# Half of x loaded already transposed, small inputs packed, and the loads at the start put over two queues

## The chip, the cores and the metric

One NeuronCore of one Trainium2 chip runs the whole program. Its engines work side by side and each in its own fixed order: TensorE (PE, matmuls and transposes), VectorE (DVE), ScalarE (ACT), GpSimd (POOL) and SyncE (SP, which here only issues DMAs). The metric is the device time of one execution in microseconds; the time of a version is the median of its runs.

## The reference, cut to what matters

Two pre-norm residual layers on x of 256 positions by 2048 features, all float32. Layer 0 is sliding-window attention with sinks, layer 1 a sparse attention with three branches. The change touches the first things that layer 0 computes: the norm, the projection, and the rotation tables.

```
def rmsnorm(x, g):
    y = xf * lax.rsqrt(jnp.mean(xf * xf, axis=-1, keepdims=True) + NORM_EPS)
    return y * g
def mixer_a(h, w_in, sinks, w_out, cos, sin):
    q, k, v, z = jnp.split(h @ w_in, ...)
    q, k = apply_rope(q, cos, sin), apply_rope(k, cos, sin)   # first 16 of 64 dims
    o = banded_attention(q, k, v, A_WINDOW, A_QBLOCK, sinks)
    return (o * jax.nn.silu(z)) @ w_out
for i in range(2):
    x = x + mixer(rmsnorm(x, norm_w[i]), ...)
return rmsnorm(x, final_norm_w)
```

## The kernel before, in words

**Matmuls.** Each projection multiplies h (256 x 2048) by a weight matrix, over 16 K-tiles of 128 features. A float32 number is split in two parts, hi and lo, which TensorE takes at the speed of its fp32r type, and a product takes three matmuls: hi by hi, lo by hi, hi by lo. Weights come in steps of 512 KB (`load`, line 544): two K-tiles by 512 columns in a tile `raw`, of which there are four. `split` (line 549) makes the parts: ACT copies `raw` to `w_hi`, DVE subtracts and writes `w_lo` (three buffers each). A step then has 12 matmuls of 128x512, six for each half of the positions, into the banks `acc0` and `acc1`.

**The first block.** Steps 0 to 7 compute keys and values (96 matmuls). Step i needs the two K-tiles 2i and 2i+1 of h transposed, features on partitions. `hT_pair` (line 523) makes them: PE transposes two K-tiles of x in four transposes into a bank `xT`, ACT multiplies by the norm weight `gT` and writes the hi part into `hT`, DVE writes the lo part. The row factor of the norm is left out here and multiplied in behind the projection. The banks `xT` come from a ring of two (`t_bank`, line 357), so a third pair's transposes wait until ACT and DVE have read the first pair. `first_block` (line 862) calls `hT_pair` one step ahead, places the squares for the norm (`square`, ACT, line 502) at steps 4 to 7, and behind them the row factor: `scales` (DVE and a power on POOL) and `scale_rows` (two transposes into `rbc`).

**Loads at the start.** SP issues constants `cst` (identity matrix and rope frequencies), norm weights `nw`, then x in column blocks of 512 (`load_x`, line 386; two DMAs of 256 KB each, one for each half of the positions) in turn with the weights of steps 0 to 3. POOL issues positions and sinks. DVE and ACT compute the rope tables from them before the first weights are split.

**What sets the order.** Nothing runs as written: every call is recorded (`Plan.record`), given a price (`_price`, line 165) and dependencies, and a list scheduler (`Plan.order`) emits each engine's instructions in the order of its own simulated time. The engines then keep that order on the chip, and wait for exact semaphores. Dependencies between recorded calls are found by boxes: a view that is sliced keeps the box of its first slice when it is rearranged and sliced again. DMAs take one of eight semaphores in turn, and a DMA waits until the eighth before it has landed.

Of the kernel before, what the change touches and what calls it, by code (L numbers as in the profile page):

```python
# [163 lines left out]
def _price(eng, method, args, kw, out, ins):  # L164

    n = math.prod(out.shape[1:]) if out is not None else 0
    if eng == "PE":
        lhs = args[1] if len(args) > 1 else kw["lhsT"]
        r = lhs.dtype == F32R
        if lhs.dtype == BF16:  # L170
            return (n / 1.2 + 2, 0)
        if method == "transpose":
            return (out.shape[-1] * (1 if r else 2) / 2.4 + 2, 0)
        if r:
            return (max(n, 256) / 2.4 + 2, 0)
        return (n * (4 if out.shape[0] > 64 else 2) / 2.4 + 2, 0)
    if method == "dma_start":
        return (1050 if eng == "POOL" else 60, 2200)
    ptrs = sum(isinstance(kw.get(k), View) for k in ("scale", "bias", "scalar", "scalar1"))
    ptrs += sum(isinstance(a, View) and math.prod(a.shape[1:]) == 1 and n > 2 for a in args[1:])  # L180
    psum = any(v.base.psum for v in ins)
    if eng == "ACT":
        return (0.833 * n + (51 if psum else 93) + 93 * ptrs + (93 if "accum_out" in kw else 0), 0)
    if eng == "DVE":
        fast = method in ("tensor_copy", "tensor_scalar") and not psum
        m = max(n, *(math.prod(v.shape[1:]) for v in ins)) if ins else n / 2
        return ((0.52 if fast else 1.042) * m + 69 + 61 * ptrs + 10, 0)
    return (1.667 * n + 185 + (300 if kw.get("op") == OP.pow else 0), 0)
# [148 lines left out]


@with_exitstack
def trunk(ctx: ExitStack, tc: tile.TileContext, x, positions, norm_w, final_norm_w,  # L340
          a_w_in, a_sinks, a_w_out, b_w_in, kc_pos, kc_w1, kc_w2, vc_pos, vc_w1, vc_w2,
          b_w_out, consts, out):
    nc = tc.nc
    plan = Plan()
    PE, ACT, DVE, POOL, SP = (Engine(plan, n, e) for n, e in (
# [24 lines left out]
    DVE.memset(warm, 0.0)  # L370
    ACT.activation(warm, warm, AF.Sin)
    ps = s_bank("idle")
    for _ in range(9):
        PE.matmul(ps, idle[:, 0:P], idle, start=True, stop=True)


    pos_i = sb.tile([P, NT], I32, name="pos_i")
    POOL.dma_start(pos_i, dram(positions, 0, [[1, P], [P, NT]]))
    cst = sb.tile([P, P + 8], F32, name="cst")
    SP.dma_start(cst, dram(consts, 0, [[CW, P], [1, P + 8]]))  # L380
    ident = cst[:, 0:P]
    nw = sb.tile([32, 512], F32, tag="q32", name="nw", bufs=2)[:, 0:P]
    SP.dma_start(nw, dram(norm_w, 0, [[P, 32], [1, P]]))
    xt = [sb.tile([P, D], F32, name=f"x{t}") for t in range(NT)]

    def load_x(j):
        for t in range(NT):
            SP.dma_start(xt[t][:, j * NB:(j + 1) * NB], dram(x, t * P * D + j * NB, [[D, P], [1, NB]]))

    load_x(0)  # L390
    sinks = sb.tile([P, 32], F32, name="sinks")
    POOL.dma_start(sinks, dram(a_sinks, 0, [[0, P], [1, 32]]))

# [6 lines left out]
    posf = sb.tile([P, NT], F32, name="posf")  # L400
    DVE.tensor_copy(posf, pos_i)
    ang = sb.tile([P, NT, 8], F32, name="ang")
    for t in range(NT):
        DVE.tensor_scalar(ang[:, t], cst[:, P:P + 8], posf[:, t:t + 1], None, op0=OP.mult)
    red = sb.tile([P, 2, NT, 8], F32, name="red")
    rnd = sb.tile([P, 2, NT, 8], F32, name="rnd")
    for i, shift in enumerate((0.0, 0.25)):
        DVE.tensor_scalar(rnd[:, i], ang, 1.0 / (2.0 * math.pi), shift, op0=OP.mult, op1=OP.add)
        DVE.tensor_scalar(rnd[:, i], rnd[:, i], MAGIC, None, op0=OP.add)
        DVE.tensor_scalar(rnd[:, i], rnd[:, i], -MAGIC, None, op0=OP.add)  # L410
        src = ang
        for c in TWO_PI:
            DVE.scalar_tensor_tensor(red[:, i], rnd[:, i], -c, src, op0=OP.mult, op1=OP.add)
            src = red[:, i]
        if i:
            DVE.tensor_scalar(red[:, i], red[:, i], math.pi / 2, None, op0=OP.add)
# [4 lines left out]
    ACT.activation(sn[:, :, 1, :], red[:, 0], AF.Sin)
    ACT.activation(cs[:, :, 0, :], red[:, 1], AF.Sin)
    DVE.tensor_copy(cs[:, :, 1, :], cs[:, :, 0, :])
    DVE.tensor_scalar(sn[:, :, 0, :], sn[:, :, 1, :], -1.0, None, op0=OP.mult)

# [22 lines left out]
    nsink = sb.tile([P, 32], F32, name="nsink")  # L448
    DVE.tensor_scalar(nsink, sinks, -1.0, None, op0=OP.mult)

    gT = sb.tile([P, 32], F32, name="gT")
    tb = t_bank("nwT")
# [69 lines left out]

    def hT_pair(i, hT, j):

        tb = t_bank("xT")
        for k in range(2):
            for t in range(NT):
                PE.transpose(tb[:, 2 * k + t, :], xt[t][:, (2 * j + k) * P:(2 * j + k + 1) * P], ident)
        src = [tb[:, 2 * k:2 * k + 2, :].rearrange("p a b -> p (a b)") for k in range(2)]
# [14 lines left out]
    def load(st):  # L544
        raw = sb.tile([P, 1024], F32, tag="raw", name="raw", bufs=4)
        st.raw = raw
        st.dma(raw)

    def split(st):
        n = st.cols  # L550
        plan.early = FIRST
        st.hi, st.lo = st.room() if hasattr(st, "room") else (
            sb.tile([P, 1024], F32R, tag=tag, name=tag, bufs=3) for tag in ("w_hi", "w_lo"))
        parts = 2 if st.idx < 2 else 1
        for c in range(parts):
# [763 lines left out]
def _consts():  # L1319
# [10 lines left out]
    for g in range(NG):  # L1330
# [25 lines left out]
```

## Time and profile before

| | us |
|---|---|
| median of 3 runs | 799.94 (799.88 to 800.97) |
| profiled execution, time | 801.18 |
| its span, first to last instruction | 799.5 |
| PE busy | 783.0 (98%) |
| DVE busy | 553.8 (69%) |
| ACT busy | 479.1 (60%) |
| POOL busy | 125.5 (16%) |
| HBM read and written | 125.91 MB and 2.10 MB |

Engines overlap, so the busy times don't add up to the span. A matmul's busy time includes its way through the array; the pace of a row of them is read from their starts. The granted clock in the profile is what the throttle reports; at the start of a program, before it has reported anything, it reads 1.00, and the pace of the matmuls tells more.

### The profile page before, as it was taken

To read this page: it belongs to the slowest core of one execution; us is meant where nothing else is said; L and a number is where in the kernel's file an instruction comes from. 1 tells how busy PE (TensorE), PEld (TensorE's weight loads), DVE (VectorE), ACT (ScalarE), POOL (GpSimd) and SP (SyncE) were. 2 spreads that over 40 slices of the span, in tenths; PEclk is the share of its full clock that TensorE was granted. 3 is DMA by queue.
4 is the path that set the end of the run, shared out by engine and by line. 5 is a ranking of instruction groups with operands and counts; after the bars stand their busy time and mean duration, and the time that the engine had idled before them with its cause. 6 is when DMAs were issued, how large, how long until landed. Compare 5 with 4: busy or idle time off the path is not lost.

```text
span 799.5 us, 11784 instructions
## 1 busy us (share of the span) xinstructions
PE 783.0 (98%) x4092; PEld 631.8 (79%) x4092; DVE 553.8 (69%) x1148; ACT 479.1 (60%) x963; POOL 125.5 (16%) x169
## 2 busy tenths in 40 slices
PE   7999999999999999999999999999999999999995
PEld 4888878788788788888878887778868768777884
DVE  5657958858779655556756478858959868885572
ACT  6658657557476445554756486667658748654452
POOL 2102311213023000020101021111211021120110
PEclk9999999999999999999999999999999999999999
DMA  8655454654653555566667653544444444364652
GB/s 271 186 181 162 131 185 129 183 159 117 180 178 132 177 185 185 182 192 172 197 204 218 184 159 106 159 109 130 132 131 134 109 127 133 109 208 131 189 181 105
DMA packets 85995, 128.77 MB, mean 161 GB/s; under 512 B 6178, under 2 KB 43265, under 8 KB 85808
## 3 DMA queue, kind: packets, MB, share of 16 engines
q1 hardware_dynamic: 85536, 126.72, 52.4%
q0 software_dynamic: 400, 1.30, 0.6%
q8 instruction: 32, 0.52, 0.3%
q14 instruction: 27, 0.22, 0.1%
HBM read 125.91 MB, written 2.10 MB: 160 GB/s over the span
## 4 chain that ended last, share of the span: by engine, by line
PE 92%; DVE 3%; issue 2%; ACT 1%; DMA 1%; POOL 1%; SPq 0%; ACTq 0%; POOLq 0%; DVEq 0%
PE acc L217 75%; PE pv L217 5%; PE s L217 4%; PE pT L217 4%; PE qT L217 1%; DVE w_lo L217 1%; PE xT L217 1%; DMA raw<-in_a_w_in 1%; DVE sm L217 1%; ACT w_hi L217 1%; PE gates L217 1%; PE pcT L217 0%; PE kT L217 0%; PE mlp L217 0%; POOL rope L217 0%
## 5 line engine op out<-in xcount | busy, mean ns | idle before, releaser
L217 DVE TENSOR_TENSOR w_lo<-raw,w_hi 128x1024 fp32r<-128x1024 f32 (+1 forms) x231 | 294.0, 1275 | 154.8 <-ACT w_hi L217 151.7
L217 ACT ACTIVATE w_hi<-raw 128x1024 fp32r<-128x1024 f32 (+1 forms) x231 | 242.0, 1050 | 186.0 <-PE acc L217 149.3
L217 PE MATMUL acc<-w_hi,hT 128*128 128x512 f32 x768 | 247.6, 398 | 2.3 <-ACT w_hi L217 1.7
L217 PE MATMUL acc<-hT,w_hi 128*128 128x512 f32 x512 | 186.4, 399 | 0.0
L217 PEld LDWEIGHTS acc<-w_hi,hT 128*128 128x128 f32 x768 | 142.9, 189 | 37.9 <-issue 4.9
L217 PE MATMUL acc<-w_lo,hT 128*128 128x512 f32 x384 | 152.1, 396 | 0.0
L217 PE MATMUL acc<-hT,w_lo 128*128 128x256 f32 x512 | 143.7, 283 | 0.0
L217 PEld LDWEIGHTS acc<-hT,w_hi 128*128 128x128 f32 x512 | 96.2, 188 | 21.3 <-issue 3.2
L217 PEld LDWEIGHTS acc<-hT,w_lo 128*128 128x128 f32 x512 | 96.6, 189 | 0.7
L217 PE MATMUL acc<-w_hi,aT_hi 128*128 128x512 f32 x236 | 92.9, 394 | 0.8 <-ACT aT_hi L217 0.8
L217 PE MATMUL acc<-w_hi,aT_lo 128*128 128x512 f32 x236 | 92.6, 392 | 0.2 <-DVE aT_lo L217 0.2
L217 PE MATMUL acc<-w_lo,aT_hi 128*128 128x512 f32 x236 | 92.1, 391 | 0.0
L217 PEld LDWEIGHTS acc<-w_lo,hT 128*128 128x128 f32 x384 | 72.7, 189 | 18.5 <-issue 4.9
L217 ACT ACTIVATE sm<-sm,nmb 128x128 f32<-128x128 f32 (+1 forms) x128 | 56.9, 445 | 15.7 <-DVE nmb L217 15.1
L217 DVE CUSTOM_DVE_ANT_0 sm<-s,mask 128x128 f32<-128x128 f32 (+1 forms) x128 | 44.1, 349 | 20.6 <-PE s L217 20.4
L217 PEld LDWEIGHTS acc<-w_hi,aT_hi 128*128 128x128 f32 x236 | 44.3, 188 | 13.4 <-issue 2.4
L217 POOL TENSOR_TENSOR sm<-sm,denb 128x512 f32<-128x512 f32 (+1 forms) x16 | 29.3, 1832 | 151.2 <-DVE mx L217 60.8
L217 PEld LDWEIGHTS acc<-w_lo,aT_hi 128*128 128x128 f32 x236 | 44.3, 188 | 9.7 <-issue 0.8
L217 PEld LDWEIGHTS acc<-w_hi,aT_lo 128*128 128x128 f32 x236 | 44.3, 188 | 9.2 <-DVE aT_lo L217 0.5
L217 PE MATMUL s<-kTB,qT 128*128 128x272 f32 x192 | 39.2, 295 | 0.0
L217 PE MATMUL pT<-cst,sm 128*128 128x128 f32 x256 | 37.9, 275 | 0.5 <-DVE sm L217 0.2
L217 PEld LDWEIGHTS s<-kTB,qT 128*128 128x128 f32 x192 | 31.8, 188 | 7.4 <-issue 3.2
(187 smaller groups left out, 885.3 us busy)
## 6 DMA issues: line engine op xcount, KB each, us to landing
raw<-in_b_w_in SPq DMA_DIRECT2D x88, 512.0 KB, 3.7
raw<-in_a_w_in SPq DMA_DIRECT2D x72, 512.0 KB, 3.6
raw<-in_a_w_out SPq DMA_DIRECT2D x32, 512.0 KB, 3.6
raw<-in_b_w_out SPq DMA_DIRECT2D x32, 512.0 KB, 4.2
x<-in_x SPq DMA_DIRECT2D x8, 256.0 KB, 7.0
raw<-in_b_cmp_k_w SPq DMA_DIRECT2D x4, 512.0 KB, 3.8
raw<-in_b_cmp_v_w SPq DMA_DIRECT2D x4, 512.0 KB, 3.8
out<-x SPq DMA_DIRECT2D x4, 512.0 KB, 3.1
```

The source lines that it names most:

```text
L217: return getattr(eng.real, method)(*[real(a) for a in args], **{k: real(a) for k, a in kw.items()})
```

## The change

Half of x (K-tiles 0 to 7) comes from the host once more as `xT`, laid out by feature, and is loaded into `xf`, a tile in the room of `aT_hi`, in four DMAs of 256 KB, two K-tiles each. `hT_pair` takes those K-tiles from `xf` in place of transposes; x itself is still loaded whole. Norm weights, sinks, positions and frequencies come packed in one input `small` (128 x 74). ACT's queue issues `small` and the two halves of step 0's weights; all else stays on SP, and POOL issues none of them. POOL builds the identity matrix. The squares and the rope tables are tied to later steps. A tenth idle matmul stands at the start, and the planner's price for a DMA that is not issued by POOL is 450 in place of 60 ns.

```
-        return (1050 if eng == "POOL" else 60, 2200)
+        return (1050 if eng == "POOL" else 450, 2200)
...
-    for _ in range(9):
+    for _ in range(10):
         PE.matmul(ps, idle[:, 0:P], idle, start=True, stop=True)
...
-    POOL.dma_start(pos_i, dram(positions, 0, [[1, P], [P, NT]]))
-    SP.dma_start(cst, dram(consts, 0, [[CW, P], [1, P + 8]]))
-    SP.dma_start(nw, dram(norm_w, 0, [[P, 32], [1, P]]))
+    small_t = sb.tile([P, SMALL], F32, name="small")
+    ACT.dma_start(small_t, small)
+    gT = small_t[:, 0:32]
...
+    xf = sb.tile([P, KT * S], F32, tag="aT_hi", name="xf")[:, 0:XT * S].rearrange("p (k s) -> p k s", k=XT)
...
-    load_x(0)
-    POOL.dma_start(sinks, dram(a_sinks, 0, [[0, P], [1, 32]]))
+    def load_xf(k0, k1):
+        SP.dma_start(xf[:, k0:k1, :], dram(xT, k0 * S, [[XT * S, P], [S, k1 - k0], [1, S]]))
+    ident = sb.tile([P, P], F32, name="ident")
+    POOL.memset(ident, 1.0)
...
+    def rope_tables(later):
+        DVE.tensor_scalar(nsink, sinks, -1.0, None, op0=OP.mult).deps.add(later.i)
...
-    PE.transpose(tb[:, 0, 0:32], nw, ident[0:32, 0:32])
-    copy(gT, tb[:, 0, 0:32])
...
-        tb = t_bank("xT")
...
+        if i == 0 and 2 * j < XT:
+            src = [xf[:, 2 * j + k, :] for k in range(2)]
+        else:
+            tb = t_bank("xT")
...
+        if st.idx == 0:
+            for k in range(2):
+                ACT.dma_start(raw[:, k * NB:(k + 1) * NB],
+                              dram(a_w_in[0], k * P * A_IN + 2048, [[A_IN, P], [1, NB]]))
+            return
...
-                    square(0, t, i - 4)
+                    square(0, t, (i - 2) % 4).deps.add(steps[i + 1].ops[0].i)
+            if i == 5:
+                rope_tables(steps[i + 1].ops[1])
...
-        if i + 1 < 4:
-            load_x(i + 1)
+        if 2 * i < XT:
+            load_xf(2 * i, 2 * i + 2)
...
+        if i < 4:
+            load_x((i + 2) % 4)
```

The emitted order moves at three places. The first is SP's queue at the start. Before, constants, norm weights and x stand ahead of the first weights:

```order
L217 DMA cst<-in_consts 128x136
L217 DMA nw<-in_norm_w 32x128
L217 DMA x_67<-in_x 128x512
L217 DMA x_68<-in_x 128x512
L217 DMA raw<-in_a_w_in 128x2x512
```

After that a pair of x and one `raw` took turns. Now the queue begins with the first `xf` and the weights of steps 1 to 3, and goes on so:

```order
L217 DMA x_67<-in_x 128x512
L217 DMA x_68<-in_x 128x512
L217 DMA x_67<-in_x 128x512
L217 DMA x_68<-in_x 128x512
L217 DMA xf<-in_xT 128x512
L217 DMA x_67<-in_x 128x512
L217 DMA x_68<-in_x 128x512
L217 DMA x_67<-in_x 128x512
L217 DMA x_68<-in_x 128x512
L217 DMA raw<-in_a_w_in 128x2x512 x3
L217 DMA xf<-in_xT 128x512 x2
L217 DMA raw<-in_a_w_in 128x2x512 x9
```

The second `xf` stands behind half of x, and the third and fourth behind the rest of x and the weights of steps 4 to 6.

The second place is ACT in the first block (`junk` are the squares, `w_hi` the weights' hi parts, `hT` the hi parts of h). Before:

```order
L217 ACTIVATE hT<-xT,gT 128x256
L217 ACTIVATE w_hi<-raw 128x512 x2
L217 ACTIVATE hT<-xT,gT 128x256 x3
L217 ACTIVATE junk,ssq_103<-x_67 128x512
L217 ACTIVATE junk,ssq_103<-x_68 128x512
L217 ACTIVATE w_hi<-raw 128x512 x2
L217 ACTIVATE hT<-xT,gT 128x256 x2
```

Now:

```order
L217 ACTIVATE w_hi<-raw 128x512 x3
L217 ACTIVATE w_hi<-raw 128x1024
L217 ACTIVATE w_hi<-raw 128x512
L217 ACTIVATE hT<-xf,small 128x256 x8
L217 ACTIVATE hT<-xT,small 128x256 x3
L217 ACTIVATE w_hi<-raw 128x1024
L217 ACTIVATE hT<-xT,small 128x256 x3
```

The weights of steps 0 to 2 are copied first; then all eight K-tiles of `xf` stand in a row, and behind them the first transposed ones and the weights of step 3. DVE's lo parts follow in the same order.

The third place is PE at its third group of transposes (numbers tell the banks apart: `acc0` and `acc1` are the two halves of the positions, `xT` with a number one bank of transposes). Before, the third and fourth group stood inside step 0:

```order
L217 MATMUL acc0_221<-w_hi_70,hT_63 128x512
L217 MATMUL acc0_221<-w_lo_71,hT_63 128x512
L217 MATMUL xT_240<-cst_91,x0_67 128x128
L217 MATMUL xT_240<-cst_91,x1_68 128x128
L217 MATMUL xT_240<-cst_91,x0_67 128x128
L217 MATMUL xT_240<-cst_91,x1_68 128x128
L217 MATMUL acc0_221<-w_hi_70,hT_63 128x512 x2
```

Now `xT_196` and `xT_201` (K-tiles 8 to 11) are transposed before the first matmul, and `xT_259`, which takes the bank of `xT_196`, stands in step 1, behind nine of its twelve matmuls:

```order
L217 MATMUL acc1_219<-w_hi_180,hT_63 128x512 x2
L217 MATMUL acc1_219<-w_lo_183,hT_63 128x512
L217 MATMUL xT_259<-ident_87,x0_67 128x128
L217 MATMUL xT_259<-ident_87,x1_68 128x128
L217 MATMUL xT_259<-ident_87,x0_67 128x128
L217 MATMUL xT_259<-ident_87,x1_68 128x128
L217 MATMUL acc1_219<-w_hi_180,hT_63 128x512 x2
L217 MATMUL acc1_219<-w_lo_183,hT_63 128x512
```

Sixteen of 32 transposes of layer 0 are gone; of those left, eight stand before the first matmul as before, four in step 1 and four in step 2. In the rest of the program the engines' orders are the same but for a few places where two neighbours have changed turns.

## Rows read from the trace of the kernel before

**Rows 1.** The page's chain of work that ended last, by engine.

```profile
PE 92%; DVE 3%; issue 2%; ACT 1%; DMA 1%; POOL 1%; SPq 0%; ACTq 0%; POOLq 0%; DVEq 0%
```

**Rows 2.** Busy time by stretch: start:end length, then each engine's us (instructions), clock, DMA.

```profile
0.00:10.07 10.07, 6.42 (x18) 2.76 (x18) 3.30 (x25) 4.38 (x12) 4.16 (x16) 1.00 0.70 183
10.07:38.87 28.80, 28.29 (x122) 22.83 (x123) 19.72 (x34) 19.98 (x41) 2.32 (x4) 1.00 0.78 249
38.87:780.00 741.13, 737.43 (x3906) 597.58 (x3905) 526.42 (x1080) 450.65 (x904) 117.92 (x149) 1.00 0.53 159
```

**Rows 3.** PE in order of time: start us, length, what, count, idle before and releaser.

```profile
6.79 1.54 PE L217 MATMUL xT<-cst,x 128*128 128x128 f32 x6 [0.65 <-DMA x<-in_x]
10.07 1.22 PE L217 MATMUL acc<-w_hi,hT 128*128 128x512 f32 x2 [1.75 <-ACT w_hi L217]
11.80 0.79 PE L217 MATMUL acc<-w_hi,hT 128*128 128x512 f32 x1 [0.50 <-DVE hT L217]
...
17.46 0.40 PE L217 MATMUL acc<-w_lo,hT 128*128 128x512 f32 x1
...
41.61 0.46 PE L217 MATMUL kT<-identr,kstack 128*128 128x128 f32 x4
```

**Rows 4.** The chain of waits in the first 60 us: start, length, what, count.

```profile
13.87 0.85 PE acc L217 x2
...
26.98 0.44 PE xT L217 x4
...
29.48 12.29 PE acc L217 x54
```

**Rows 5.** SP's first DMA issue, in order of time.

```profile
0.81 0.38 SPq L217 DMA_DIRECT2D cst<-in_consts  x1
```

**Rows 6.** Busy time by stretch as in rows 2; the last two columns are DMA share and GB/s.

```profile
1.50:2.00 0.50, 0.50 (x2) 0.15 (x1) 0.26 (x1) 0.50 (x1) 0.50 (x1) 1.00 0.32 47
0.00:4.00 4.00, 2.74 (x7) 1.01 (x8) 0.77 (x4) 1.49 (x2) 2.85 (x11) 1.00 0.41 87
4.00:8.00 4.00, 3.35 (x12) 1.75 (x10) 1.88 (x16) 1.53 (x5) 1.31 (x7) 1.00 0.80 164
8.00:12.00 4.00, 1.75 (x5) 0.70 (x4) 2.58 (x8) 3.29 (x9) 0.00 (x0) 1.00 1.05 403
12.00:18.00 6.00, 6.00 (x20) 4.87 (x21) 4.02 (x8) 5.72 (x15) 0.00 (x0) 1.00 1.05 387
```

**Rows 7.** DMA queues between 4 and 8 us: packets, MB, share of the 16 DMA engines.

```profile
q1 hardware_dynamic: 334, 0.64, 45.5%
q0 software_dynamic: 57, 0.02, 34.8%
```

**Rows 8.** DMA issues of the first 60 us: size, median us from issue to landing.

```profile
pos_i<-in_positions POOLq DMA_DIRECT2D x1, 1.0 KB, 4.7
sinks<-in_a_sinks POOLq DMA_DIRECT2D x1, 16.0 KB, 5.8
```

**Rows 9.** ACT, POOL and DVE in order of time, 21 to 25 us.

```profile
21.55 0.62 ACT L217 ACTIVATE junk<-x 128x512 f32<-128x512 f32 x1
...
22.16 1.05 ACT L217 ACTIVATE w_hi<-raw 128x1024 fp32r<-128x1024 f32 x1
...
23.11 1.20 ACT L217 ACTIVATE hT<-xT,gT 128x256 fp32r<-128x256 f32 x3
...
23.27 1.79 POOL L217 TENSOR_TENSOR r<-ms,nhalf 128x2 f32<-128x2 f32 x1 [17.96 <-DVE ms L217]
...
24.38 0.87 DVE L217 SCALAR_TENSOR_TENSOR hT<-xT,gT,hT 128x256 fp32r<-128x256 f32 x2
```

**Rows 10.** PE's last matmul, in order of time.

```profile
790.46 0.39 PE L217 MATMUL acc<-w_lo,aT_hi 128*128 128x512 f32 x1
```

**Rows 11.** Two stretches at the end, columns as in rows 2.

```profile
795.40:795.60 0.20, 0.00 (x0) 0.00 (x0) 0.00 (x0) 0.00 (x0) 0.00 (x0) 1.00 0.78 307
795.60:795.80 0.20, 0.00 (x0) 0.00 (x0) 0.00 (x0) 0.00 (x0) 0.00 (x0) 0.58 1.14 471
```

More of the change, by code (lines that the diff above doesn't have):

```diff
@@ L339, in trunk @@
 @with_exitstack
-def trunk(ctx: ExitStack, tc: tile.TileContext, x, positions, norm_w, final_norm_w,
-          a_w_in, a_sinks, a_w_out, b_w_in, kc_pos, kc_w1, kc_w2, vc_pos, vc_w1, vc_w2,
-          b_w_out, consts, out):
+def trunk(ctx: ExitStack, tc: tile.TileContext, x, final_norm_w, a_w_in, a_w_out, b_w_in, kc_pos, kc_w1, kc_w2, vc_pos, vc_w1, vc_w2,
+          b_w_out, consts, small, xT, out):
     nc = tc.nc
@@ L363, in copy @@
     def copy(out, in_, scale=1.0):
-        ACT.activation(out, in_, AF.Copy, scale=scale)
+        return ACT.activation(out, in_, AF.Copy, scale=scale)
     idle = sb.tile([P, NB], BF16, name="idle")
@@ L372, in trunk @@
     ps = s_bank("idle")
-    for _ in range(9):
+    for _ in range(10):
         PE.matmul(ps, idle[:, 0:P], idle, start=True, stop=True)
-    pos_i = sb.tile([P, NT], I32, name="pos_i")
-    POOL.dma_start(pos_i, dram(positions, 0, [[1, P], [P, NT]]))
-    cst = sb.tile([P, P + 8], F32, name="cst")
-    SP.dma_start(cst, dram(consts, 0, [[CW, P], [1, P + 8]]))
-    ident = cst[:, 0:P]
-    nw = sb.tile([32, 512], F32, tag="q32", name="nw", bufs=2)[:, 0:P]
-    SP.dma_start(nw, dram(norm_w, 0, [[P, 32], [1, P]]))
+    small_t = sb.tile([P, SMALL], F32, name="small")
+    ACT.dma_start(small_t, small)
+    gT = small_t[:, 0:32]
+    sinks = small_t[:, 32:64]
+    pos_i = small_t[:, 64:66].bitcast(I32)
+    inv_freq = small_t[:, 66:74]
     xt = [sb.tile([P, D], F32, name=f"x{t}") for t in range(NT)]
+    xf = sb.tile([P, KT * S], F32, tag="aT_hi", name="xf")[:, 0:XT * S].rearrange("p (k s) -> p k s", k=XT)
     def load_x(j):
@@ L388, in load_x @@
             SP.dma_start(xt[t][:, j * NB:(j + 1) * NB], dram(x, t * P * D + j * NB, [[D, P], [1, NB]]))
-    load_x(0)
-    sinks = sb.tile([P, 32], F32, name="sinks")
-    POOL.dma_start(sinks, dram(a_sinks, 0, [[0, P], [1, 32]]))
+    def load_xf(k0, k1):
+        SP.dma_start(xf[:, k0:k1, :], dram(xT, k0 * S, [[XT * S, P], [S, k1 - k0], [1, S]]))
+    ident = sb.tile([P, P], F32, name="ident")
+    POOL.memset(ident, 1.0)
+    for sign in (1, -1):
+        POOL.affine_select(out=ident, in_=ident, pattern=[[-sign, P]], compare_op=OP.is_ge, fill=0.0,
+                           base=0, channel_multiplier=sign)
     identr = sb.tile([P, P], F32R, name="identr")
@@ L397, in trunk @@
     DVE.memset(nhalf, -0.5)
[L400 to L416, printed above, removed]
@@ L417, in trunk @@
-    lim = float(np.nextafter(np.float32(math.pi), np.float32(0)))
-    DVE.tensor_scalar(red, red, lim, -lim, op0=OP.min, op1=OP.max)
+    nsink = sb.tile([P, 32], F32, name="nsink")
     cs = sb.tile([P, NT, 2, 8], F32, name="cs")
     sn = sb.tile([P, NT, 2, 8], F32, name="sn")
[L421 to L424, printed above, removed]
+    def rope_tables(later):
+        DVE.tensor_scalar(nsink, sinks, -1.0, None, op0=OP.mult).deps.add(later.i)
+        posf = sb.tile([P, NT], F32, name="posf")
+        DVE.tensor_copy(posf, pos_i).deps.add(later.i)
+        ang = sb.tile([P, NT, 8], F32, name="ang")
+        for t in range(NT):
+            DVE.tensor_scalar(ang[:, t], inv_freq, posf[:, t:t + 1], None, op0=OP.mult)
+        red = sb.tile([P, 2, NT, 8], F32, name="red")
+        rnd = sb.tile([P, 2, NT, 8], F32, name="rnd")
+        for i, shift in enumerate((0.0, 0.25)):
+            DVE.tensor_scalar(rnd[:, i], ang, 1.0 / (2.0 * math.pi), shift, op0=OP.mult, op1=OP.add)
+        DVE.tensor_scalar(rnd, rnd, MAGIC, None, op0=OP.add)
+        DVE.tensor_scalar(rnd, rnd, -MAGIC, None, op0=OP.add)
+        src = ang[:, None].to_broadcast([P, 2, NT, 8])
+        for c in TWO_PI:
+            DVE.scalar_tensor_tensor(red, rnd, -c, src, op0=OP.mult, op1=OP.add)
+            src = red
+        DVE.tensor_scalar(red[:, 1], red[:, 1], math.pi / 2, None, op0=OP.add)
+        lim = float(np.nextafter(np.float32(math.pi), np.float32(0)))
+        DVE.tensor_scalar(red, red, lim, -lim, op0=OP.min, op1=OP.max)
+        ACT.activation(sn[:, :, 1, :], red[:, 0], AF.Sin)
+        ACT.activation(cs[:, :, 0, :], red[:, 1], AF.Sin)
+        DVE.tensor_copy(cs[:, :, 1, :], cs[:, :, 0, :])
+        DVE.tensor_scalar(sn[:, :, 0, :], sn[:, :, 1, :], -1.0, None, op0=OP.mult)
@@ L447, in trunk @@
     mflat = mask.rearrange("p a b -> p (a b)")
[L448 to L452, printed above, removed]
-    PE.transpose(tb[:, 0, 0:32], nw, ident[0:32, 0:32])
-    copy(gT, tb[:, 0, 0:32])
     urgent, queue = deque(), deque()
@@ L503, in square @@
         junk = sb.tile([P, NB], F32, tag="q32", name="junk", bufs=2)
-        ACT.activation(junk, xt[t][:, j * NB:(j + 1) * NB], AF.Square, accum_out=ssq[i][:, t, j:j + 1])
+        return ACT.activation(junk, xt[t][:, j * NB:(j + 1) * NB], AF.Square, accum_out=ssq[i][:, t, j:j + 1])
     def rstd(i, ts=slice(0, NT)):
@@ L523, in hT_pair @@
     def hT_pair(i, hT, j):
-        tb = t_bank("xT")
[L526 to L529, printed above, removed]
+        if i == 0 and 2 * j < XT:
[3 more added lines that the diff above has]
+            for k in range(2):
+                for t in range(NT):
+                    PE.transpose(tb[:, 2 * k + t, :], xt[t][:, (2 * j + k) * P:(2 * j + k + 1) * P], ident)
+            src = [tb[:, 2 * k:2 * k + 2, :].rearrange("p a b -> p (a b)") for k in range(2)]
         g = [gT[:, i * KT + 2 * j + k:i * KT + 2 * j + k + 1] for k in range(2)]
@@ L546, in load @@
         st.raw = raw
+        if st.idx == 0:
+            for k in range(2):
+                ACT.dma_start(raw[:, k * NB:(k + 1) * NB],
+                              dram(a_w_in[0], k * P * A_IN + 2048, [[A_IN, P], [1, NB]]))
+            return
         st.dma(raw)
@@ L556, in split @@
             part = slice(c * n // parts, (c + 1) * n // parts)
-            copy(st.hi[:, part], st.raw[:, part])
-            DVE.tensor_sub(st.lo[:, part], st.raw[:, part], st.hi[:, part])
+            st.ops = (copy(st.hi[:, part], st.raw[:, part]),
+                      DVE.tensor_sub(st.lo[:, part], st.raw[:, part], st.hi[:, part]))
         plan.early = 0
@@ L1333, in _consts, with _small @@
     return c
-_INS = ["x", "positions", "norm_w", "final_norm_w", "a_w_in", "a_sinks", "a_w_out", "b_w_in",
+XT = 8
+SMALL = 74
+def _small(norm_w, a_sinks, positions):
+    parts = [norm_w.reshape(-1, P).T, np.broadcast_to(a_sinks.reshape(1, -1), (P, 32)),
+             np.ascontiguousarray(positions.reshape(NT, P).T).view(np.float32),
+             np.broadcast_to(np.asarray(INV_FREQ, np.float32), (P, 8))]
+    return np.ascontiguousarray(np.concatenate([np.ascontiguousarray(a) for a in parts], axis=1))
+_INS = ["x", "final_norm_w", "a_w_in", "a_w_out", "b_w_in",
         "b_cmp_k_pos", "b_cmp_k_w1", "b_cmp_k_w2", "b_cmp_v_pos", "b_cmp_v_w1", "b_cmp_v_w2", "b_w_out"]
@@ L1347 @@
     data["consts"] = _consts()
+    data["small"] = _small(*(np.asarray(inputs[name]) for name in ("norm_w", "a_sinks", "positions")))
+    data["xT"] = np.ascontiguousarray(data["x"].reshape(S, KT, P)[:, :XT].transpose(2, 1, 0).reshape(P, XT * S))
     for name, a in data.items():
```

## The prediction, made before the result was known

> **What bounds the kernel now.** I read the chain of waits first: 92% of the span is TensorE's own work [rows 1]. Then busy time by stretch: from 38.87 us to 780 us PE is busy 737.43 of 741.13 us, but it works only 6.42 of the first 10.07 [rows 2]. In the middle nothing moves but what is PE work, and the change leaves that alone; what counts is when the first block (steps 0 to 7, keys and values) ends, since all later matmuls follow it without a gap. In PE's own order of time the first matmul starts at 10.07, and the `kT` transposes at 41.61 come 12 matmuls after the block's last [rows 3]. A full-pace matmul takes 12.29 / 54 = 0.2276 us [rows 4], so the block ends at 41.61 - 12 x 0.2276 = 38.9. The start runs at half pace: two matmuls in 0.85 at 13.87 [rows 4], which is the 1.2 GHz level, until 17.46, where the pace doubles, 5.66 us after the last gap ended at 11.80 [rows 3].
>
> The DMA engines are the other limit of the start: they move 87 and 164 GB/s in the first two stretches of 4 us, then 403 and 387 with a share of 1.05, that is, full [rows 6]. Between 4 and 8 us the software queue, with 0.02 MB of positions and sinks, holds 34.8% of the DMA engines and the hardware queue only 45.5% [rows 7]; positions and sinks land 4.7 and 5.8 us after their issue [rows 8].
>
> **The change part by part.** The sum is made on the profiled execution (801.18 us, span 799.5 and 1.68 around it, 1.24 above the median); I add the difference to the median, 799.94.
>
> *The transposes.* Sixteen of layer 0's 32 go. The eight ahead of the first matmul are as many as before; of the 24 behind it 16 go, 8 at half pace (0.21 us) and 8 at 0.44 / 4 = 0.11 [rows 4], together 2.6 us of PE time. That is the gain if PE never waits.
>
> *The wait that comes in.* `xT_259` stands in step 1 behind nine of its matmuls, and takes the bank of `xT_196`. That bank is free when ACT and DVE have read K-tiles 8 and 9. Both have them in their queues behind all eight K-tiles of `xf`, so behind the landing of the fourth `xf` DMA, which SP issues after all of x and the weights of steps 4 to 6. PE is in order: behind `xT_259` wait the rest of step 1 and steps 2 to 7, though steps 2's weights are long split. So the block's end follows from that landing, L.
>
> From L to the block's end: ACT has four hi parts to make (K-tiles 6 to 9). Three take 1.20 [rows 9], of which I read 0.37 apart and 0.46 for the last: 3 x 0.37 + 0.46 = 1.57, and about 0.1 for K-tile 5 just before. DVE's lo parts of K-tiles 8 and 9 follow, 0.87 [rows 9]. PE goes on at L + 2.55. Then 8 transposes x 0.11 = 0.88, 75 matmuls (3 of step 1, 72 of steps 2 to 7) x 0.2276 = 17.07, and two `rbc` transposes 0.22: 18.17. The weights of step 3, which stand behind K-tile 10 on ACT, are just in time: 0.37 + 1.05 for their copy, and DVE's part after it, beside 9 matmuls and four transposes.
>
> *Squares and rope tables.* They come later: the last two squares stand behind the weights of step 8 on ACT, whose buffer is free when step 5 is done, 24 matmuls before the end, 5.7 us with `rbc`. Behind them: 1.05 for that copy, two squares x 0.62, the power on POOL 1.79 [rows 9], and some 0.9 for two sines and five tiny DVE operations (an estimate), 5.0 in all. The `rbc` transposes want the result 0.9 before the end, at 4.8, so PE waits about 0.3 (bounds 0 and 1). Moved off the start, the rope tables free ACT and DVE before the first split; that gains nothing, since L decides.
>
> So the block ends at L + 2.55 + 18.17 + 0.3 = L + 21.0, and the change costs L + 21.0 - 38.9 = L - 17.9.
>
> *When does L come?* Ahead of it, and with it, the engines carry: `small` 37 KB, step 0's weights 512, the four `xf` 1024, weights of steps 1 to 6 3072, x 2048: 6693 KB, 6.85 MB. ACT's queue carries 0.56 MB of that, and early, so which queue has it doesn't matter: the engines are full with one queue [rows 6]. Earliest: the first bytes flow within 1.5 to 2.0 us for an issue at 0.81 [rows 5, 6], and 6.85 MB at 403 GB/s from 1.75 on end at 18.75: +0.85 us. Latest: the old start unchanged, 4 x 87 + 4 x 164 + 4 x 403 + 6 x 387 = 4.94 MB by 18 us [rows 6], the last 1.91 at 387: 22.9, +5.0. I take a value between, from what is removed: by 8 us the old 1.00 MB, and 34.8% of 4 us back from the software queue (1.39 us x 403 = 0.56), and about 0.9 us of earlier start, since the first large DMA takes SP's first turn in place of its third, x 403 = 0.36, and half of the 19.7% in which neither queue moved [rows 7], 0.16: 2.08 MB. Then 1.61 until 12, and 3.16 MB at 387: L = 20.2. The change costs 20.2 - 17.9 = **+2.3 us: 802.2**.
>
> *At nothing:* `nwT`, `gT` and the constants' loads go, all done before 10.07 beside other waits. The identity on POOL (one fill, two selections) is ready long before the x that it transposes. The issues on ACT (0.4 each, as SP's [rows 5]) delay the table load, and the first split waits for weights anyway. The tenth idle matmul ends before x is there. The 1.09 MB of additional loads is in L. Later stages are the same PE work, and PE's 3.7 us of waiting there [rows 2] hang on local chains.
>
> **The rivals.** *The clock falls in the gap.* The second pair of x lands with 2.92 MB, at 10.1; 8 transposes at half pace later, at 11.8, come 21 matmuls, 13.3 of them at half pace for 5.66 us, the rest in 1.75, so PE reaches `xT_259` at 19.2 and waits until 22.75, 3.5 us. If the clock falls there, another 5.66 us at half pace cost 2.8: 805.0. Against it: at the end PE's last matmul starts at 790.46 [rows 10], and the granted clock reads 1.00 (2.4 GHz) until 795.6, then goes to half [rows 11], about 4.8 us of idling; the gap is shorter, but it grows if the clock rises earlier, and one end of one execution is little to go by. The Trainium skill, "TensorE: Matmul & The Clock Gate", section "Why this matters for your kernels", advises against idle gaps between bursts of matmuls, since one that is long enough puts the clock back; by that rule this rival would be the forecast. The trace has one such fall, after a gap longer than this one.
>
> *The features come in time (not slower).* If L comes before 19.2 - 2.55 = 16.7, PE doesn't wait, and the block ends at 19.2 + 18.17 + 0.3 = 37.7: -1.2, 798.7; with x's pair as early as the bounds allow, about 1 us less, 797.7. Any L before 17.9 is a gain. It needs 6.85 MB in 15 us, 460 GB/s, or a fourth `xf` that overtakes what stands ahead of it. For it: 471 GB/s shows in one fifth of a microsecond [rows 11]. Against it: 403 is the best over 4 us [rows 6].
>
> *The start stays as slow as it is.* If the software queue was not what held the hardware queue back, L goes to 22.9: 805.0.
>
> **How the numbers follow.** The forecast's case, L between 18.75 and 22.9 with the clock kept, has 62%, its own range 800.8 to 805.0; the clock's fall 20%; features in time 10%; something in later stages that this reading doesn't show 8%. What a measurement here can tell from no change is about 0.2%, 1.6 us. In the forecast's case L must be above 19.5 for that, two thirds of it: with the clock's fall and a share of the rest, slower 0.66; same 0.28, from a low L and most of the early features; faster 0.06. The range, 800.4 to 806.2, leaves out most of the early features at one end and a clock's fall on top of a slow start at the other.
>
> **What would show it.** Right: PE waits 3 to 5 us within step 1, released by DVE's `hT`, at about 22.7; ACT idles 6 us or more between K-tiles 3 and 4, released by an `xf` DMA; the `kT` transposes start near 43.9 in place of 41.61; the hardware queue moves over 300 GB/s from 3 us on. Wrong: no wait of PE between the first matmul and `rbc`, or an `xf` DMA that lands with the ones issued long before it. A half pace after that wait would be the clock's rival.

## The result, and the profile after

The changed kernel takes 809.47 us (median of 4 runs, 808.53 to 809.70), the kernel before, run beside it, 800.37: ratio 1.0108, 95% interval 1.0093 to 1.0123. It is slower, as forecast, but by 9.1 us and not by 2.3. The profiled runs, 809.42 (span 807.7) and 801.18, differ by 8.2, since the profiled run of the kernel before lies 0.8 above its median.

PE in order of time, as in [rows 3]: start, length, what, count, idle before and releaser.

```profile
10.98 1.94 PE L217 MATMUL xT<-ident,x 128*128 128x128 f32 x8 [5.96 <-DMA x<-in_x]
...
18.08 0.39 PE L217 MATMUL acc<-w_lo,hT 128*128 128x512 f32 x1
25.99 1.09 PE L217 MATMUL xT<-ident,x 128*128 128x128 f32 x4 [7.53 <-issue]
26.73 1.20 PE L217 MATMUL acc<-w_hi,hT 128*128 128x512 f32 x2
...
31.43 0.74 PE L217 MATMUL acc<-w_hi,hT 128*128 128x512 f32 x2
...
46.07 0.38 PE L217 MATMUL rbc<-ident,rh 128*128 128x128 f32 x2
...
49.48 0.45 PE L217 MATMUL kT<-identr,kstack 128*128 128x128 f32 x4
```

The `kT` transposes start 7.87 us later than in [rows 3], so nearly the whole loss lies before them. PE stands still for 7.5 us ahead of `xT_259` (25.99), and what follows runs at half pace: two matmuls in 1.20 at 26.73, in 0.74 at 31.43. The same stretch by busy time, columns as in [rows 2], shows the granted clock, the third number from the end, ahead of DMA share and GB/s.

```profile
7.50:8.00 0.50, 0.00 (x0) 0.00 (x0) 0.40 (x1) 0.50 (x3) 0.00 (x0) 0.60 1.05 389
...
14.50:18.00 3.50, 3.50 (x17) 2.90 (x16) 0.88 (x2) 0.91 (x2) 0.00 (x0) 1.00 1.06 408
18.00:21.00 3.00, 0.47 (x3) 0.04 (x1) 0.00 (x0) 0.00 (x0) 0.00 (x0) 1.00 1.05 385
21.00:21.50 0.50, 0.00 (x0) 0.00 (x0) 0.00 (x0) 0.00 (x0) 0.00 (x0) 0.75 0.34 119
21.50:26.00 4.50, 0.01 (x1) 0.04 (x1) 2.56 (x6) 3.44 (x8) 0.00 (x0) 0.50 0.02 6
26.00:31.00 5.00, 5.00 (x15) 4.02 (x16) 3.96 (x6) 2.55 (x5) 0.00 (x0) 0.50 0.33 105
31.50:36.00 4.50, 4.50 (x22) 3.73 (x21) 2.10 (x3) 3.51 (x8) 0.00 (x0) 1.00 0.37 116
```

PE does nothing from 18.5 on; the clock goes from 1.00 (2.4 GHz) to 0.50 (1.2 GHz) between 21.0 and 21.5 and is back only after 31. It had fallen once before, between 7.5 and 8, in the 5.96 us in which PE waits for x; the half pace behind that ends at 14.4 and is no part of the loss, since in [rows 3] it lasts until 17.46. What PE waits for shows on ACT, in order of time, in one row of DVE, and in SP's issue of the last two `xf` loads with the time that the second of them took to land:

```profile
15.18 0.91 ACT L217 ACTIVATE hT<-xf,small 128x256 fp32r<-128x256 f32 x2 [3.94 <-DMA xf<-in_xT]
22.56 1.70 ACT L217 ACTIVATE hT<-xf,small 128x256 fp32r<-128x256 f32 x4 [6.47 <-DMA xf<-in_xT]
24.17 1.18 ACT L217 ACTIVATE hT<-xT,small 128x256 fp32r<-128x256 f32 x3
```

```profile
25.02 0.88 DVE L217 SCALAR_TENSOR_TENSOR hT<-xT,small,hT 128x256 fp32r<-128x256 f32 x2 [0.24 <-ACT hT L217]
```

```profile
15.17 1.02 SPq L217 DMA_DIRECT2D xf<-in_xT  x2
...
xf<-in_xT SPq DMA_DIRECT2D x1, 256.0 KB, 7.3
```

ACT idles 6.47 us, until the third `xf` load is there: it landed at 22.54. The fourth, issued at 15.85, landed 7.3 us later, at 23.16, before ACT had made the two K-tiles of the third. So ACT makes four K-tiles from `xf` in a row and then two from the bank of `xT_196`. DVE's last part of it ends at 25.90, and PE goes on at 25.99. Last, the DMA engines, columns as in [rows 6]:

```profile
4.00:8.00 4.00, 1.02 (x4) 0.20 (x2) 0.40 (x1) 1.06 (x3) 0.00 (x0) 0.95 1.05 404
...
9.00:15.00 6.00, 4.01 (x15) 3.57 (x16) 3.12 (x5) 2.24 (x4) 0.00 (x0) 0.55 1.00 339
...
21.00:22.00 1.00, 0.00 (x0) 0.00 (x0) 0.00 (x0) 0.00 (x0) 0.00 (x0) 0.63 0.20 72
```

From 4 to 8 us they move 404 GB/s, where they moved 164 before [rows 6]. From 9 to 15 it is only 339, and from 21 on a thin rest.

### The profile page after: what moved, and what is told of

Read it like the earlier page. It is cut to its first block, busy times and chain, and to the rows that moved or that the text cites. A ratio compares the mean times of both kernels' runs of the same rounds, so it can differ in the third digit from the quotient of the medians.

```text
span 807.7 us, 11742 instructions
## 1 busy us (share of the span) xinstructions
PE 780.3 (97%) x4076; PEld 630.8 (78%) x4076; DVE 553.4 (69%) x1143; ACT 479.4 (59%) x962; POOL 123.9 (15%) x170
## 4 chain that ended last, share of the span: by engine, by line
PE 91%; issue 3%; DVE 2%; DMA 1%; ACT 1%; POOL 1%; SPq 0%; ACTq 0%; POOLq 0%; DVEq 0%
PE acc L217 74%; PE pv L217 5%; PE s L217 4%; PE pT L217 4%; PE qT L217 1%; DMA x<-in_x 1%; DVE w_lo L217 1%; PE xT L217 1%; DVE sm L217 1%; PE gates L217 1%; ACT w_hi L217 0%; PE pcT L217 0%; PE kT L217 0%; PE mlp L217 0%; POOL rope L217 0%
## 5 line engine op out<-in xcount | busy, mean ns | idle before, releaser
L217 PEld LDWEIGHTS acc<-hT,w_hi 128*128 128x128 f32 x512 | 96.2, 188 | 21.3 <-issue 3.2
L217 DVE CUSTOM_DVE_ANT_0 sm<-s,mask 128x128 f32<-128x128 f32 (+1 forms) x128 | 44.0, 348 | 20.6 <-PE s L217 20.4
L217 PE MATMUL pT<-ident,sm 128*128 128x128 f32 x256 | 37.9, 275 | 0.5 <-DVE sm L217 0.2
```

The lines of the kernel that those rows point to most:

```text
L217: return getattr(eng.real, method)(*[real(a) for a in args], **{k: real(a) for k, a in kw.items()})
```

## The experiments

All ratios are to the kernel before. My theory: the loss is the late landing of the last `xf` loads, which the planner's order makes, and behind the wait a half pace that the wait brings. In the source, `xf` is sliced and rearranged before its K-tiles are cut out of it, so its box is that of all eight. The planner therefore takes every load and read of `xf` to touch all eight K-tiles: it lets the loads wait for each other, and even the first copy wait for all four. Its order follows from that, though the waits that end up in the program are exact.

**Exact boxes.** Each K-tile is cut from the tile itself:

```
-    xf = sb.tile([P, KT * S], F32, tag="aT_hi", name="xf")[:, 0:XT * S].rearrange(...)
+    xf = sb.tile([P, KT * S], F32, tag="aT_hi", name="xf")
...
-        SP.dma_start(xf[:, k0:k1, :], ...
+        SP.dma_start(xf[:, k0 * S:k1 * S].rearrange("p (k s) -> p k s", k=k1 - k0), ...
...
-            src = [xf[:, 2 * j + k, :] for k in range(2)]
+            src = [xf[:, (2 * j + k) * S:(2 * j + k + 1) * S] for k in range(2)]
```

> The changed kernel, but each slice of xf is cut from the tile itself, so that the planner sees which K-tiles a load writes and a copy reads (before, every slice kept the box of all eight). The planned order is then: SP issues the four xf loads first, alternating with the weights of steps 1 to 3, then x; ACT and DVE take K-tiles 0 to 7 as they land; PE starts with matmuls in place of eight transposes. Theory A (the loss is the late landing of the fourth xf, made by the planner's order): at about 400 GB/s 3.07 MB end near 10.3 us, so no wait of PE after its first matmul; it starts near 8 us, half pace for about 6 us, 82 more matmuls at 0.2276 and 16 transposes at 0.11 put the block's end near 34.6, against 38.9 of the kernel before: about 797 in the profiled run, some 795.5 to 797 timed, ratio 0.995. Rival B (the engines are full anyway, so whatever is issued earlier makes another load late by as much): PE waits for x or for weights of steps 4 to 6 instead, total 803 or more. Rival C (the additional work on ACT and DVE, not the order, holds PE): K-tiles 0 to 7 still end over 3 us behind their landing, 801 to 805.

Measured: 795.94 us, ratio 0.9947 (0.9934 to 0.9961): by the ratios 12.9 us below the changed kernel. PE in order of time:

```profile
7.25 1.20 PE L217 MATMUL acc<-w_hi,hT 128*128 128x512 f32 x4 [1.54 <-ACT w_hi L217]
...
9.61 1.20 PE L217 MATMUL acc<-w_hi,hT 128*128 128x512 f32 x4 [0.70 <-ACT w_hi L217]
...
21.66 1.20 PE L217 MATMUL acc<-w_hi,hT 128*128 128x512 f32 x4 [0.32 <-ACT w_hi L217]
...
35.77 0.46 PE L217 MATMUL kT<-identr,kstack 128*128 128x128 f32 x4
```

The long wait is gone; 0.70 and 0.32 are what is left behind the first matmul. The pace is full from the first matmul on: four in 1.20, where the changed kernel has two in 1.20 behind its wait. Theory A holds in place and size; B and C fall.

**Only the loads moved.** SP issues `xf` 1 to 3 right behind `xf` 0; PE, ACT, DVE and POOL keep the changed kernel's order word for word:

```
+        ops = [op for op in self.order() if op not in self.xf_loads[1:]]
+        at = ops.index(self.xf_loads[0]) + 1
+        for op in ops[:at] + self.xf_loads[1:] + ops[at:]:
```

> The changed kernel with one thing moved: SP issues xf 1, 2 and 3 right behind xf 0, ahead of the weights and of x. All other engines keep the order of the changed kernel word for word. Theory A (the fourth xf's landing sets the wait at xT_259): x lands 0.75 MB later, so the first transposes start near 12.9 in place of 10.98; PE reaches xT_259 near 20.4 and does not wait; block end 20.4 + 18.2 + 0.3 = 38.9, the kernel before's, so 801 in the profiled run, ratio 1.000 and 8 us under the changed kernel. Rival B (the order on ACT and DVE and the bank of xT_196 hold PE, whenever xf lands): a wait of 3 us or more stays at the same place, 804 to 808.

Measured: 801.29, ratio 1.0010 (1.0001 to 1.0018). PE reaches `xT_259` at 20.33 and doesn't wait:

```profile
12.90 1.94 PE L218 MATMUL xT<-ident,x 128*128 128x128 f32 x8 [7.20 <-DMA x<-in_x]
...
20.33 0.60 PE L218 MATMUL xT<-ident,x 128*128 128x128 f32 x4
...
41.25 0.46 PE L218 MATMUL kT<-identr,kstack 128*128 128x128 f32 x4
```

So it is the landing, and not the order on ACT and DVE or the bank, that holds PE; the three numbers forecast (12.9, 20.4, 801) are met. What lies between this and the exact boxes, 5.3 us, is the order on the other engines and of SP's remaining loads, which were not told apart.

**The pace behind the wait.** 34 idle matmuls fill PE's wait in the changed kernel (the trace has records of 33):

```
+                    if (i, j) == (0, 6):
+                        op.ahead = keep_busy     # 34 idle matmuls ahead of xT_259
```

> The changed kernel with 34 more idle matmuls on PE just ahead of the transposes that wait 7.5 us (34 at 0.213 us are 7.3 us at full pace, so they end just before the wait does); nothing else differs. Theory A (after the gap PE works 5.4 us at half pace, so 2.7 us of the loss are the clock's): the granted clock stays 1.00 through the gap and 26 to 31.4 us, block end 2.7 earlier, 806.7, ratio to before about 1.007. Rival B (the half pace is not the gap's doing, or what is behind it waits for weights anyway): 809 to 810, ratio 1.011.

Measured: 807.17, ratio 1.0082 (1.0068 to 1.0096). PE in order of time, and one stretch of busy time:

```profile
18.35 7.51 PE L383 MATMUL idle<-idle 128*128 128x512 bf16 x33
26.02 0.63 PE L217 MATMUL xT<-ident,x 128*128 128x128 f32 x4 [0.17 <-issue]
...
46.97 0.46 PE L217 MATMUL kT<-identr,kstack 128*128 128x128 f32 x4
```

```profile
26.00:31.00 5.00, 4.98 (x26) 4.17 (x27) 4.65 (x8) 3.95 (x8) 0.00 (x0) 1.00 0.36 108
```

PE goes on at the same time, but the clock reads 1.00 and 26 matmuls and transposes fit where 15 did; `kT` comes 2.51 us sooner (49.48 - 46.97). The half pace follows from the gap and costs 2.1 (by the ratios) to 2.5 us (by `kT`).

**The landing where the forecast had it.** SP issues the last two `xf` ahead of the weights of steps 5 and 6:

```
+        last = self.xf_loads[2:]          # issued behind the weights of step 4
+        for op in ops[:at] + last + ops[at:]:
```

> The changed kernel with the last two xf loads moved on SP ahead of the weights of steps 5 and 6 (1.05 MB less in front of them; all else in the same order). It puts the landing of the fourth xf where the prediction had it: 22.5 - 1.05 MB / 387 GB/s = 19.8 in place of 22.5. From the landing to PE's next instruction the changed kernel took 3.4 us, so PE goes on near 23.2, after a gap of 4.7 us in place of 7.5. Theory A (the block follows the landing one for one, and the clock does not fall in the shorter gap): 2.8 us from the landing and 2.7 from the clock, 803.9. Theory A' (the clock falls in this gap too): 806.6, half pace for some 5 us behind it. Rival B (the landing is not the cause): 808 to 809.5.

Measured: 806.05, ratio 1.0065 (1.0053 to 1.0078). ACT, PE, and the clock in the gap:

```profile
19.26 1.70 ACT L218 ACTIVATE hT<-xf,small 128x256 fp32r<-128x256 f32 x4 [3.85 <-DMA xf<-in_xT]
```

```profile
22.69 1.08 PE L218 MATMUL xT<-ident,x 128*128 128x128 f32 x4 [4.15 <-issue]
...
46.36 0.46 PE L218 MATMUL kT<-identr,kstack 128*128 128x128 f32 x4
```

```profile
21.50:22.00 0.50, 0.00 (x0) 0.00 (x0) 0.28 (x1) 0.50 (x3) 0.00 (x0) 0.69 0.06 25
```

A' it is: the clock falls in this shorter gap too. The fourth `xf` was issued at 13.86 and landed 6.0 us later, at 19.9, close to the 20.2 of the forecast. `kT` comes 4.75 us later than in [rows 3]; the prediction's sum with its own rival, the clock's fall, gives 19.9 - 17.9 + 2.8 = 4.8. This is the run that decides on that rival.

**The same, with the pace kept.** 19 idle matmuls in that gap (the trace has records of 18).

> The last two xf loads 1.05 MB earlier, and 19 idle matmuls (4.05 us at full pace) in the 4.15 us that PE waits then. Theory A (the wait and the clock add up, and with the clock kept the block follows the landing as the prediction's sum has it): 2.7 us under the same kernel without the idle matmuls (806.05), 803.3, ratio 1.003; of the 2.3 to 3 us that are left over the kernel before, 1.4 are the landing at 19.3 (less 17.9) and 0.8 that two more K-tiles stand behind it. Rival B (the half pace behind the gap hides waits that come up when it goes): 804.5 or more.

Measured: 803.77, ratio 1.0041 (1.0029 to 1.0054); 2.3 less (1.9 by the ratios), where 2.7 were expected.

```profile
18.39 1.71 ACT L218 ACTIVATE hT<-xf,small 128x256 fp32r<-128x256 f32 x4 [3.81 <-DMA xf<-in_xT]
```

```profile
18.90 4.28 PE L388 MATMUL idle<-idle 128*128 128x512 bf16 x18
23.01 0.60 PE L218 MATMUL xT<-ident,x 128*128 128x128 f32 x4
...
43.94 0.46 PE L218 MATMUL kT<-identr,kstack 128*128 128x128 f32 x4
```

Here the third `xf` let ACT go on at 18.39, 0.9 us sooner than without the idle matmuls. From ACT's going on to PE's it took 3.43 us in the run before (19.26 to 22.69), so PE could have gone on at 21.8; the idle matmuls held it until 23.01. By this reckoning the miss is the filler's own, and the two runs are no clean measure of the pace. From 23.01 to `kT` it takes 20.93 us, the prediction's 18.17 and 12 x 0.2276.

**The rate of the DMA engines.** Only the second `xf` moves, from between the halves of x to behind the first.

> The changed kernel with only the second xf load moved, from between the two halves of x to right behind the first xf; the third and fourth stay last. Theory A (the DMA rate of 339 GB/s between 9 and 15 us comes with an xf load among those of x, and is why the fourth landed later than forecast): 385 GB/s or more throughout, the landing 0.7 us earlier, PE goes on near 25.3, 808.7, ratio 1.010. Rival B (the rate does not hang on that place): still 320 to 360 in that stretch, 809.5, ratio 1.011.

Measured: 807.28, ratio 1.0082 (1.0068 to 1.0096), less than both expected. ACT, then the stretch of busy time:

```profile
21.04 1.70 ACT L218 ACTIVATE hT<-xf,small 128x256 fp32r<-128x256 f32 x4 [8.33 <-DMA xf<-in_xT]
```

```profile
9.00:15.00 6.00, 3.31 (x12) 3.05 (x13) 4.56 (x8) 3.52 (x7) 0.00 (x0) 0.50 1.06 388
```

388 GB/s, a landing 1.5 us earlier, and no thin rest. Four runs have the second `xf` in its old place. Three of them are slow there: 339 GB/s in the changed kernel, 323 with its wait filled, 348 with the last two `xf` earlier. The fourth, with the same loads in the same order as the third and idle matmuls that begin only at 18.9, is not. The rows of these two:

```profile
9.00:15.00 6.00, 4.30 (x15) 3.81 (x16) 2.89 (x5) 2.43 (x6) 0.00 (x0) 0.51 1.02 348
...
9.00:15.00 6.00, 3.90 (x14) 3.45 (x15) 3.72 (x7) 3.25 (x6) 0.00 (x0) 0.50 1.05 385
```

So the place alone doesn't set the rate, though every slow stretch has it. In these five runs the thin rest goes with the slow stretch: from 21 to 22 us 72, 133 and 64 GB/s are moved in the three slow ones, 8 and 2 in the other two. Why the rate is low in some runs stays open.

**The change without `xf`.** x is loaded and transposed as before, all else of the change stays:

```
-        if i == 0 and 2 * j < XT:
-            src = [xf[:, 2 * j + k, :] for k in range(2)]
...
-        if 2 * i < XT:
-            load_xf(2 * i, 2 * i + 2)
+        if i + 1 < 4:
+            load_x(i + 1)
```

> The change without xf: x is loaded and transposed on PE as before, in the order of before; the packed small inputs, step 0's weights on ACT's queue, the identity on GpSimd, the later squares and rope tables, ten idle matmuls and the planner's price of an issue stay. Theory A (the loss is xf's alone; the rest of the change takes work off the start): first matmul near 8.5 to 9 in place of 10.07, block end 1 to 1.5 us earlier, 799 in the profiled run, 798 to 799.5 timed, ratio 0.998. Rival B (the packed inputs, the second queue or the later squares cost something by themselves): 802 or more.

Measured: 796.28, ratio 0.9950 (0.9937 to 0.9962), a gain of 4.3 us where 0.5 to 2 were expected. PE in order of time:

```profile
7.58 0.73 PE L217 MATMUL acc<-w_hi,hT 128*128 128x512 f32 x2 [0.44 <-ACT hT L217]
9.46 0.50 PE L217 MATMUL acc<-w_hi,hT 128*128 128x512 f32 x1 [1.15 <-DVE hT L217]
...
36.66 0.46 PE L217 MATMUL kT<-identr,kstack 128*128 128x128 f32 x4
```

The first matmul comes 2.5 us sooner than in [rows 3], and at full pace at once, two matmuls in 0.73 where [rows 3] has them in 1.22 and full pace from 17.46: that I had not counted. Three runs take it apart.

*The kernel before, with four idle matmuls in its 1.75 us wait:*

> The kernel before with four more idle matmuls on PE just ahead of its first weights matmul, where it waits 1.75 us (four at 0.43 us are 1.7 us); nothing else differs. Theory A (the start of the kernel before is slow because PE stays at half pace until 17.46, and that follows from the gaps in its work; most of what the change without xf gained, 4.9 us, is the earlier pace): pace doubles by about 11 to 13, some 10 to 14 matmuls at 0.2276 in place of 0.42, 2 to 3 us gained, 797 to 798.5, ratio 0.997. Rival B (the gain without xf is the earlier data alone): first matmul still near 10.07, pace still doubles after 17, 800 to 801.5.

Measured: 798.50, ratio 0.9978 (0.9967 to 0.9989).

```profile
7.51 0.92 PE L217 MATMUL xT<-cst,x 128*128 128x128 f32 x6 [1.86 <-DMA x<-in_x]
8.22 1.91 PE L384 MATMUL idle<-idle 128*128 128x512 bf16 x4
10.07 1.22 PE L217 MATMUL acc<-w_hi,hT 128*128 128x512 f32 x2
...
12.13 0.40 PE L217 MATMUL acc<-w_lo,hT 128*128 128x512 f32 x1
...
39.02 0.46 PE L217 MATMUL kT<-identr,kstack 128*128 128x128 f32 x4
```

```profile
8.00:12.00 4.00, 3.50 (x11) 1.38 (x10) 2.83 (x11) 3.57 (x11) 0.00 (x0) 0.57 1.05 401
```

The first matmul stays at 10.07, full pace comes at 12.1, and `kT` 2.59 earlier. By the ratio, closing this small gap is worth 1.8 us. That all of the 2.59 come from it is not shown: in this execution the transposes at 7.51, ahead of the idle matmuls, already run at full pace (six in 0.92, in [rows 3] in 1.54), and the clock falls behind them all the same (0.57 from 8 to 12). So the two traces differ in pace before the edit can act.

*Without `xf`, squares and rope tables back in the start:*

> The change without xf, with squares and rope tables where the kernel before has them (in the start, among the copies of the first steps). Theory A (moving them matters, since ACT is on the path while the first weights and features are made): first matmuls later by the 0.6 us squares that stand ahead of the first copies on ACT, one or two gaps more on PE, 797.5 to 799, so 1.5 to 2.5 us of the 4.3 gained without xf. Rival B (they lie beside waits, as the prediction held): 796 to 796.8, the same as without xf.

Measured: 798.80, ratio 0.9973 (0.9963 to 0.9983); by the ratios the move is worth 1.8 us, theory A's size.

```profile
8.80 0.73 PE L217 MATMUL acc<-w_hi,hT 128*128 128x512 f32 x2 [1.67 <-ACT hT L217]
10.45 0.79 PE L217 MATMUL acc<-w_hi,hT 128*128 128x512 f32 x1 [0.91 <-DVE hT L217]
```

The first matmul is 1.2 us later, and the one behind the next gap runs at half pace (0.79, where the run without the early tables has 0.50).

*Without `xf`, step 0's weights on SP's queue:*

> The change without xf, with step 0's weights issued by SP behind the first x, as before, in place of ACT's queue. Theory A (the second queue brings the first weights sooner): weights of step 0 are split 1 us or more later, first matmul near 9, a longer gap behind the transposes, pace doubles later: 797.5 to 799. Rival B (the engines are full with one queue, so which queue has them does not matter, as the prediction held): 796 to 796.8.

Measured: 796.18, ratio 0.9942 (0.9929 to 0.9956), the same as with two queues: rival B. The Trainium skill, "Trainium Kernel Development and Optimization", section "Key Constraints", says that DMAs issued from several engines share the same 16 DMA engines and that a second issuer only saves issue time; this run agrees.

**Improving on the exact boxes.** First 13 idle matmuls at the start for ten; then also step 4's weights issued ahead of the half of x that only the squares want.

> The exact boxes with 13 idle matmuls at the start in place of ten: PE is idle there from 5.71 to 7.25, and three more at 0.43 us reach 7.0. Theory A (the gap delays the pace): pace doubles by 9.6 in place of 11.1, six to eight matmuls at 0.2276 in place of 0.42, 1.2 us less at most, of which some goes into later waits for the weights of step 4 (ACT took them at 20.5, PE waited 0.3): 794.8 to 795.5. Rival B (what is ahead waits for the weights of step 4 anyway): 795.9, no change.

> As the one before, and SP issues the weights of step 4 ahead of the second half of x's loads (the K-tiles that came by feature, which only the squares want), 1.05 MB sooner, 2.7 us at 387 GB/s. Theory A (the weights of step 4 are next in the chain): no wait of PE at 21 us, 0.3 to 1.2 us under the one before: 794 to 795. Rival B (ACT's order holds them: their copy stands behind K-tiles 8 to 15): no difference between the two.

Measured: 795.85, ratio 0.9941 (0.9928 to 0.9955), and 795.64, ratio 0.9939 (0.9926 to 0.9951). Neither is told apart from the exact boxes (0.9947); there the pace was full from the first matmul on, so more idle matmuls had none to bring forward. In the second, ACT:

```profile
19.04 1.57 ACT L217 ACTIVATE hT<-xT,small 128x256 fp32r<-128x256 f32 x4 [2.07 <-PE xT L217]
20.49 2.02 ACT L217 ACTIVATE w_hi<-raw 128x1024 fp32r<-128x1024 f32 x2
```

PE's 0.32 us wait stays, at 21.61: the copy of step 4's weights follows the K-tiles from `xT` on ACT, and these wait for PE. Rival B holds in both. 795.64 is the lowest time, by the ratios 13.5 us below the changed kernel; `xf` itself, by exact boxes or left out, makes no difference that shows.

## Why the prediction was wrong, by its own steps

- **The place, right.** PE waits at `xT_259` in step 1, released through ACT and DVE by the last `xf` loads; ACT idles 6.47 us between K-tiles 3 and 4; PE's work from there to `kT` takes 20.9 us at full pace, as summed (read where the wait is filled, and no half pace comes in: 46.97 - 26.02 = 20.95).
- **L, mis-sized: 23.16 in place of 20.2.** It lies even behind the 22.9 that the prediction called the latest. Up to 8 us the estimate was near (1.97 MB against 2.08, 0.3 us). From 9 to 15 the sum took 403 and 387 GB/s, and 339 were moved: 0.34 MB, 0.9 us. With the rates as measured and the total divided by them, the last byte would have come at 21.3; the fourth `xf` landed 1.9 us behind that. The landings don't slow at the end: from 14.44 on, loads of 256 KB land 0.6 to 0.7 us after the load ahead of them. It was one load of x before that which landed 2.05 us behind its predecessor (12.39, 14.44), where the run with 385 GB/s has 0.68 (12.30, 12.98). From 22.0 to 22.5 the DMA engines move 25 GB/s, a sixteenth of 404; an estimate from these two numbers is that one of the 16 had fallen behind, and that every load waited for its share. The trace doesn't tell the engines apart, so the cause stays open.
- **L + 2.55, near: 2.83.** The third `xf` landed 0.62 us ahead of the fourth, so a little more of its second K-tile stood behind L than the 0.1 reckoned.
- **The clock kept in the gap, the step that failed in kind.** It was the forecast's case at 62%, from one fall seen at the end of the kernel [rows 10, 11]. It fell in the 7.5 us gap (filled: 2.51 us less), in a gap of 4.15 us (806.05), and already in the 5.96 us in which PE waits for x. The sign that the prediction named for it, a half pace behind the wait, is there. With that rival and the landing of the forecast the sum would have been 805.0. The rule of the Trainium skill that I weighed there ("TensorE: Matmul & The Clock Gate", "Why this matters for your kernels": no idle gaps between bursts of matmuls, or the clock goes back) should have been the forecast: these gaps agree with it.
- **The sum.** `kT` was due at 20.2 + 21.0 + 2.73 = 43.9. With 2.96 from L, 0.28 from the K-tiles, 2.51 from the clock, and without the 0.3 for `rbc` (PE went through it at 46.07 without a wait) it is 49.4; measured 49.48.
- **"At nothing", right only behind that wait.** What the change does besides `xf` is worth 4.0 (by the ratio) to 4.3 us once `xf` is out. The later squares and tables are 1.8 of that, the second queue none; the packed inputs, the identity and the tenth idle matmul were not told apart. Had the landing not decided, the forecast would have missed it by that. So `xf` in this order costs 1.0108 - 0.9950, 12.6 us.
- **The rival "the start stays as slow as it is".** Its L, 22.9, is near the one measured, but by chance: the start was not slow.
- **The faster start of the loads, right in size.** 404 GB/s from 4 to 8 us where 164 flowed, though only from 4 us on and not from 3. That it was the software queue, and not the order of the loads, no run separates.

## What to carry to other kernels

When a planner orders the work, look up which region it thinks each access touches: a view cut in the wrong order made four independent loads one, and cost 12.9 us. A wait of PE can have two prices, its length and the half pace behind it, as the gaps of 4.15 and 7.5 us had here; look for the second in the granted clock of the gap and in the length of a pair of matmuls after it, and where the wait can't go, idle matmuls in it give back the second price, as long as they don't outlast it. A total divided by a rate is a lower bound for the time of the last load: here it landed 1.9 us later.

## What the runs showed of the hardware, unexpected

- At the start, the granted clock's column can miss a half pace: in the kernel before it reads 1.00 throughout [rows 2, 6], with pairs of matmuls in 1.22 us at 10.07 and full pace from 17.46 [rows 3]; with the wait filled it reads 0.57 from 8 to 12, with the same 1.22 at 10.07. The length of a matmul tells the pace in both.
- The pace at the start differs much between runs: full pace from the first matmul on with exact boxes (7.25) and without `xf` (7.58), from 12.13 in the kernel before with its wait filled, from 17.46 without.
- The DMA engines moved 348 and 385 GB/s between 9 and 15 us with the same loads in the same order on SP (the last two `xf` earlier, without and with idle matmuls). Not settled.
